# Reciprocal square roots with a GpSimd power as first guess in a hybrid attention layer

## The chip, the cores and the metric

The kernel runs on one core of a Trainium2 chip. The metric is device time in microseconds (us) of one execution, the median of several runs. The core's engines are PE (TensorE, matrix products; PEld is its weight load), DVE (VectorE), ACT (ScalarE), POOL (GpSimd) and SP (SyncE, which issues most DMAs). Each engine takes its own instructions strictly in the order in which the built program lists them, and waits on semaphores for the others.

## The reference

One inference step of one layer, on 2048 prompt tokens and 8 sequences of 16 sample tokens, 2176 tokens of width 1024 in all. The parts that matter here are its normalisations:

```
def rms_norm(x, g):
    y = x * rsqrt(mean(x * x) + EPS);  return y * g
def l2_norm(x):
    return x * rsqrt(sum(x * x) + EPS)

h = rms_norm(x, g_in);  all projections = h @ w_in
q_a = l2_norm(q_a) * 128 ** -0.5;  k_a = l2_norm(k_a)          # DeltaNet group, 4 heads of 128
o_a = rms_norm(gated_delta(q_a, k_a, v_a, ...), g_o) * silu(z_a)
q_b, k_b, q_m = rms_norm per head of 64;  k_i = rms_norm of 32  # sparse and memory attention, indexer
o_b = attention over the 256 best keys by indexer score
o_m = attention over 256 memory tokens
y = x + concat(o_a, o_b, o_m) @ w_out
```

## The kernel before

Tokens lie on the 128 partitions, in 17 tiles; tile 0 holds the sample tokens. The tiles form five groups of 4, 4, 3, 3 and 3 (`GROUPS`). The first part of the kernel, some 1600 us long, runs eleven streams beside one another: `projections` (h times the weights, in split precision, so three products each), their posts `n_post`, `idx_post` and `head_post`, the DeltaNet stages a, b and c (`delta_a`, `delta_b`, `delta_c`, one run per group and head, b and c in two or three units of tiles), `prep` (which scales the tokens by the norm `rstd`), weight loading and splitting, and the indexer with its top-k search (`topk`). The second part, to the end, runs sparse and memory attention and the output product.

The streams are generators. `weave` takes them in turn by a planned clock: each engine has a running time, a wrapper (`Paced`, whose call stands on line 169, which is why nearly every row of the profile names L169) adds a cost for each instruction, by engine and by width, and the stream with the earliest time goes next. A DVE step on a few elements is planned at some 71 ns, a POOL product on a few elements at some 155 ns. A framework then places buffers and semaphores, and schedules within that. So the order of all engines follows from planned costs, and another cost moves it.

The helper of this study is `rsqrt(y, x, pool, tag)` on lines 297 to 308. It works on very small operands: 128 partitions by 1 to 8 elements. It makes a first guess by integer arithmetic on the bits of x (the row writes int32) and two refinement steps, eight DVE instructions that each need the one before. It is called

- in `norms` (line 325, result `rstd`, scratch `x_b`), 5 times, once a group;
- in `n_post` (line 428, `nrs`, `n_b`), 30 times, for q and k of the sparse attention and q of the memory attention; the scaled `nraw` then goes to a POOL product, `nth`;
- in `idx_post` (line 468, `irs`, `i_b`), 10 times;
- in `topk` (line 553, `sdr`, `t_b`), 15 times, once for each searched tile, for a starting threshold;
- in `memory_keys` (lines 829 and 845), 3 times;
- in `delta_a` (line 1002, `drr`, `d_b`), 20 times, for the norms of k and q of a head; `rq` is q's part;
- in `delta_c` (line 1225, `fo`, `o_b`), 44 times, for the norm of the output `o`, from its sum of squares `sso`, into `Ao`, after squaring `rq`.

POOL's own work in the first part: `wl` and `mw` (low parts of split weights), `Lm` (masked copies of a triangular matrix, two buffers, so one must wait until PE has used an earlier one), `qn` (low part of the indexer's queries), `q`, `kdb`, `nth` and some memsets. In the first part DVE also makes `Z`, `Sst`, `kw`, `cv` for the DeltaNet chain on PE, `xr` and `xl` for the projections, `score` and the top-k steps for ACT.

Of the kernel before, what the change touches and what calls it, by code (L numbers as in the profile page):

```python
# [5 lines left out]
F32 = mybir.dt.float32  # L6
F32R = mybir.dt.float32r
BF = mybir.dt.bfloat16
I32 = mybir.dt.int32
AF = mybir.ActivationFunctionType  # L10
OP = mybir.AluOpType
# [5 lines left out]
EPS = 1e-6  # L17
# [189 lines left out]
def build(tc, nc, a):  # L207
# [3 lines left out]
    V, S, G, T = (Paced(e, n, log) for e, n in ((nc.vector, "V"), (nc.scalar, "S"), (nc.gpsimd, "G"), (nc.tensor, "T")))  # L211


    cpool = ctx.enter_context(tc.tile_pool(name="const", bufs=1))
# [79 lines left out]
    xh = xpool.tile([128, 8, MAXTOK], F32R, name="xh")  # L294
    xl = xpool.tile([128, 8, MAXTOK], F32R, name="xl")

    def rsqrt(y, x, pool, tag):

        t = pool.tile([128, x.shape[-1]], F32, name=tag + "_b", tag="rsq_b" + tag)
        V.tensor_scalar(y.bitcast(I32), x.bitcast(I32), -0.5, 1597463007.0, op0=OP.mult, op1=OP.add)  # L300
        V.tensor_tensor(t, y, y, op=OP.mult)
        V.tensor_tensor(t, t, x, op=OP.mult)
        V.scalar_tensor_tensor(t, t, -10.0 / 3, t, op0=OP.add, op1=OP.mult)
        V.scalar_tensor_tensor(y, t, 5.0, y, op0=OP.add, op1=OP.mult)
        V.scalar_tensor_tensor(t, y, -27.0 / 1024, y, op0=OP.mult, op1=OP.mult)
        V.tensor_tensor(t, t, x, op=OP.mult)
        V.scalar_tensor_tensor(y, t, 0.5625, y, op0=OP.add, op1=OP.mult)

    done = dict.fromkeys(("a", "b", "c", "i", "t", "s", "n", "na", "tp", "ta", "w", "end", "m", "k", "sv", "smp", "nm", "x", "xf", "bl", "sx"), 0)
    done["xf"] = 1  # L310
# [3 lines left out]
    def norms(gi, xp):  # L314
        g0, n = GROUPS[gi]
        ss = xp.tile([128, 5, 2], F32, name="ss")
        for t in range(n):
            for e in range(2):
                xt = np_.tile([128, 512], F32, name="nraw")
                nc.sync.dma_start(xt, a["x"][(g0 + t) * 128:(g0 + t + 1) * 128, e * 512:e * 512 + 512])  # L320
                S.activation(xt, xt, AF.Square, accum_out=ss[:, t, e:e + 1])
        sm = xp.tile([128, 5], F32, name="ssm")
        V.tensor_tensor(sm[:, :n], ss[:, :n, 0], ss[:, :n, 1], op=OP.add)
        V.tensor_scalar(sm[:, :n], sm[:, :n], 1.0 / D, EPS, op0=OP.mult, op1=OP.add)
        rsqrt(rstd[:, g0:g0 + n], sm[:, :n], spool, "x%d" % n)
        done["nm"] = gi + 1
# [81 lines left out]
    def n_post(pi, t0, m, raw, npool):  # L408
        rows = slice(t0 * 128, (t0 + m) * 128)
        if pi == 3:  # L410
            nc.sync.dma_start(dst3(a["vb"][rows, :]), raw)
            nc.sync.dma_start(dst3(v_d[rows, :]), raw)
            return
        sq = npool.tile([128, 2, 256], F32, name="nth")[:, :m]
        if pi >= 4:
            S.activation(sq, raw, AF.Tanh, scale=0.5)
            yield 1
            V.scalar_tensor_tensor(raw, sq, 1.0, raw, op0=OP.add, op1=OP.mult)
            c = (pi - 4) * 256
            nc.sync.dma_start(dst3(gate_d[rows, c:c + 256]), raw)  # L420
            return
        S.activation(sq, raw, AF.Square)
        yield 1
        ss = spool.tile([128, 8], F32, name="nss")[:, :m * 4]
        V.tensor_reduce(ss, sq.rearrange("p t (h d) -> p (t h) d", d=64), axis=AX.X, op=OP.add)
        V.tensor_scalar(ss, ss, 1.0 / 64, EPS, op0=OP.mult, op1=OP.add)
        rs = spool.tile([128, 8], F32, name="nrs")[:, :m * 4]
        rsqrt(rs, ss, spool, "n%d" % m)
        r3 = raw.rearrange("p t (h d) -> p (t h) d", d=64)
        V.tensor_tensor(r3, r3, rs[:, :, None].to_broadcast([128, m * 4, 64]), op=OP.mult)  # L430
        yield 1
        gn = gains[:, pi * 64:(pi + 1) * 64]
        G.tensor_tensor(sq.rearrange("p t (h d) -> p (t h) d", d=64), r3, gn[:, None, :].to_broadcast([128, m * 4, 64]), op=OP.mult)
        nc.sync.dma_start(dst3((qn_d, kn_d, qm_d)[pi][rows, :]), sq)
        if pi == 1:
            nc.sync.dma_start(dst3(a["kb"][rows, :]), sq)
# [20 lines left out]
    def idx_post(gi, t0, m, raw, sm, final):  # L457
# [8 lines left out]
        V.tensor_scalar(ms[:, :m], ss[:, :m], 1.0 / 32, EPS, op0=OP.mult, op1=OP.add)  # L466
        rs = spool.tile([128, 2], F32, name="irs")
        rsqrt(rs[:, :m], ms[:, :m], spool, "i%d" % m)
        kn = spool.tile([128, 2, 32], F32, name="ikn")
        V.tensor_tensor(kn[:, :m], k3, rs[:, :m, None].to_broadcast([128, m, 32]), op=OP.mult)  # L470
# [511 lines left out]
    def delta_a(gi, h, R, dp):  # L982

        g0, n = GROUPS[gi]
# [18 lines left out]
        rk, rq = rr[:, :n], rr[:, n:2 * n]  # L1003
        cc = dp.tile([128, 6], F32, name="dcc")
        V.tensor_tensor(cc[:, :n], beta[:, gs, h], rk, op=OP.mult)
        bp = dp.tile([128, 6], F32, name="dbp")
        V.tensor_tensor(bp[:, :n], cc[:, :n], rk, op=OP.mult)
        nbe = dp.tile([128, 6], F32, name="dnbe")
        V.scalar_tensor_tensor(nbe[:, :n], bp[:, :n], -1.0, egc[:, gs, h], op0=OP.mult, op1=OP.mult)
        yield 1  # L1010

        Lp = dp.tile([128, 4, 128], F32, name="Lp")
        at = dp.tile([128, 4, 128], F32, name="at")
        for lo, hi in units(gi):
            m = hi - lo
# [37 lines left out]
        def full(dt):  # L1053
            return dt[:n, :16384].rearrange("t (i j) -> i t j", j=128)
# [21 lines left out]
        X = dp.tile([128, 4, 128], F32, name="X")  # L1076
        Z = dp.tile([128, 4, 128], F32, name="Z")
# [2 lines left out]
            nc.sync.dma_start(diag(Zd)[t], Zs[8 * t:8 * t + 8])  # L1080
        nc.sync.dma_start(X[:, :n], full(Xd))
        nc.sync.dma_start(Z[:, :n], full(Zd))
        R.update(Lp=Lp, at=at, X=X, Z=Z, cc=cc, nbe=nbe, rq=rq)
        yield 6000.0

    def delta_b(gi, h, lo, hi, R, dp):
# [63 lines left out]
    def delta_c(gi, h, lo, hi, R, dp):  # L1150

        g0, n = GROUPS[gi]
        q, z = (R[x][:, :n * 128].rearrange("p (t c) -> p t c", c=128) for x in "qz")
        at, rq = R["at"], R["rq"]
        Zg, kd, cv, nw = R[lo]
        m = hi - lo
        smp = g0 + lo == 0
        shp = [128, m, 128]
        sso = dp.tile([128, 3], F32, name="sso")
# [59 lines left out]

        f = dp.tile([128, 3], F32, name="fo")  # L1220
        A = dp.tile([128, 3], F32, name="Ao")
        V.tensor_tensor(f[:, :m], rq[:, lo:hi], rq[:, lo:hi], op=OP.mult)
        V.tensor_tensor(A[:, :m], f[:, :m], sso[:, :m], op=OP.mult)
        V.tensor_scalar(A[:, :m], A[:, :m], 1.0 / 16384, EPS, op0=OP.mult, op1=OP.add)
        rsqrt(f[:, :m], A[:, :m], dp, "o%d" % m)
        V.scalar_tensor_tensor(f[:, :m], f[:, :m], 128.0 ** -0.5, rq[:, lo:hi], op0=OP.mult, op1=OP.mult)
        V.tensor_tensor(o, o, f[:, :m, None].to_broadcast(shp), op=OP.mult)
# [15 lines left out]
    dp = b1.enter_context(tc.tile_pool(name="dp", bufs=2))  # L1243
# [5 lines left out]
    def stage_a():  # L1249
        for n, (gi, h, R) in enumerate(heads):  # L1250
            yield from until(lambda: done["tp"] >= 4 * n + 2 and done["t"] > gi and (n < 2 or done["c"] >= through[n - 2]))
            yield 1
            yield from delta_a(gi, h, R, dp)
            done["a"] += 1
# [7 lines left out]
    def stage_c():  # L1262
        for j, (n, lo, hi) in enumerate(pieces_):
            yield from until(lambda: done["b"] > j and done["tp"] >= 4 * n + 4)
            yield from delta_c(*heads[n][:2], lo, hi, heads[n][2], dp)
            done["c"] += 1
# [15 lines left out]
    def t_step(n, j):  # L1282
        gi, h, R = heads[n]
        parts_ = ((("k", 1, 128), ("q", 0, 0)), (("v", 2, 0), ("z", 3, 128)))[j]

        def run(w):
            if j == 0 and n >= 2:
                yield from until(lambda: done["c"] >= through[n - 2])
            yield from head_proj(n, h, gi, w, parts_, R, hp)
        return pairs(a["w_t"][2 * h + j]), run  # L1290

    def n_step(gi, pi):
        return pairs(a["w_n"][pi]), lambda w: n_piece(gi, pi, w, np_)
# [4 lines left out]
    for gi in range(len(GROUPS)):  # L1298
        t = [[t_step(4 * gi + h, 0), t_step(4 * gi + h, 1)] for h in range(4)]
        n = [n_step(gi, pi) for pi in (1, 0, 2, 3, 4, 5)]  # L1300
# [652 lines left out]
```

## Time and profile before

| | |
|---|---|
| median of 3 runs | 2352.61 us (2351.39 to 2356.84) |
| profiled execution | 2355.36 us, span 2353.5 us |
| PE busy | 2096.8 us, 89% |
| DVE busy | 1651.6 us, 70% |
| ACT busy | 1292.9 us, 55% |
| POOL busy | 419.7 us, 18% |
| mean granted clock of PE | 0.946 |

Busy time of an engine is the time in which at least one of its instructions runs; small DVE instructions overlap, so the sum of their durations is more than that. The span runs from the first to the last instruction; the execution's own time is a little longer. The granted clock is that of PE as a share of full speed.

### The profile page before, as it was taken

To read this page: it belongs to the slowest core of one execution; us is meant where nothing else is said; L and a number is where in the kernel's file an instruction comes from. 1 tells how busy PE (TensorE), PEld (TensorE's weight loads), DVE (VectorE), ACT (ScalarE), POOL (GpSimd) and SP (SyncE) were. 2 spreads that over 40 slices of the span, in tenths; PEclk is the share of its full clock that TensorE was granted. 3 is DMA by queue.
4 is the path that set the end of the run, shared out by engine and by line. 5 is a ranking of instruction groups with operands and counts; after the bars stand their busy time and mean duration, and the time that the engine had idled before them with its cause. 6 is when DMAs were issued, how large, how long until landed. Compare 5 with 4: busy or idle time off the path is not lost.

```text
span 2353.5 us, 43495 instructions
## 1 busy us (share of the span) xinstructions
PE 2096.8 (89%) x14123; PEld 1645.1 (70%) x14123; DVE 1651.6 (70%) x6571; ACT 1292.9 (55%) x3193; POOL 419.7 (18%) x494
## 2 busy tenths in 40 slices
PE   4887989788899998999899999989999999799997
PEld 3755645677688887888788888756566555467665
DVE  4765655566888787899888996777567667554552
ACT  3454545455546565676666764467456656544552
POOL 3231413211121111111111021132111111111100
PEclk9887989788999998999899999999999999999998
DMA  7688667765544555656555555368788777653212
GB/s 230 177 242 224 214 147 212 196 233 192 198 159 161 183 176 197 206 196 218 181 204 203 198 202 201 117 211 262 246 249 272 246 238 249 189 165 101 91 48 69
DMA packets 323533, 453.25 MB, mean 193 GB/s; under 512 B 81760, under 2 KB 230880, under 8 KB 303840
## 3 DMA queue, kind: packets, MB, share of 16 engines
q1 hardware_dynamic: 322976, 449.32, 59.9%
q8 instruction: 114, 1.87, 0.3%
q0 software_dynamic: 320, 1.06, 0.2%
q14 instruction: 123, 1.01, 0.1%
HBM read 344.53 MB, written 105.75 MB: 191 GB/s over the span
## 4 chain that ended last, share of the span: by engine, by line


## 5 line engine op out<-in xcount | busy, mean ns | idle before, releaser
L169 PE MATMUL pp<-wh,xh 128*128 128x256 f32 (+1 forms) x952 | 290.0, 305 | 10.6 <-ACT v L169 4.5
L169 PE MATMUL pp<-wh,xl 128*128 128x256 f32 (+1 forms) x952 | 280.6, 295 | 1.5 <-DVE xl L169 1.4
L169 PE MATMUL pp<-wl,xh 128*128 128x256 f32 (+1 forms) x952 | 280.5, 295 | 1.3 <-POOL wl L169 1.2
L169 PE MATMUL pp<-xh,wh 128*128 128x384 f32 (+1 forms) x640 | 249.5, 390 | 5.6 <-ACT q L169 3.2
L169 ACT ACTIVATE relu<-pi 128x512 f32<-128x512 f32 (+3 forms) x340 | 183.4, 545 | 125.0 <-PE pi L169 67.1
L169 PE MATMUL pp<-xh,wl 128*128 128x384 f32 (+1 forms) x640 | 242.2, 379 | 2.3 <-DMA wl<-wd2l 1.7
L169 DVE SCALAR_TENSOR_TENSOR score<-relu,w,score 128x512 f32<-128x512 f32 (+3 forms) x304 | 221.7, 731 | 29.5 <-ACT relu L169 15.0
L169 PE MATMUL pp<-xl,wh 128*128 128x384 f32 (+1 forms) x640 | 241.9, 378 | 0.0
L169 PEld LDWEIGHTS pp<-wh,xh 128*128 128x128 f32 x952 | 186.5, 196 | 17.6 <-ACT v L169 4.8
L169 PEld LDWEIGHTS pp<-wl,xh 128*128 128x128 f32 x952 | 186.3, 196 | 5.8 <-issue 2.5
L169 PEld LDWEIGHTS pp<-wh,xl 128*128 128x128 f32 x952 | 185.6, 195 | 5.1 <-DVE xl L169 2.7
L169 ACT ACTIVATE junk<-score,tf 128x1024 bf16<-128x1024 f32 (+11 forms) x126 | 142.5, 1131 | 69.8 <-DVE tf L169 47.9
L169 POOL TENSOR_TENSOR Lm<-Lp,cf 128x256 f32<-128x256 f32 (+1 forms) x120 | 85.0, 709 | 335.6 <-PE pb L169 312.2
L169 PE MATMUL pi<-kstack,qst 128*128 128x512 f32 (+3 forms) x304 | 129.6, 434 | 13.9 <-ACT relu L169 10.9
L169 PEld LDWEIGHTS pp<-xh,wh 128*128 128x128 f32 x640 | 125.4, 196 | 18.3 <-ACT q L169 3.8
L169 PEld LDWEIGHTS pp<-xh,wl 128*128 128x128 f32 x640 | 125.1, 196 | 15.6 <-issue 2.5
L169 PE MATMUL py<-woh,mixh 128*128 128x512 f32 x272 | 123.8, 455 | 11.6 <-ACT mixh L169 10.8
L169 PEld LDWEIGHTS pp<-xl,wh 128*128 128x128 f32 x640 | 125.4, 196 | 10.6 <-issue 2.5
L169 PE MATMUL py<-woh,mixl 128*128 128x512 f32 x272 | 111.4, 410 | 4.7 <-POOL mixl L169 4.5
L169 POOL TENSOR_TENSOR wl<-wr,wh 128x512 fp32r<-128x512 f32 (+1 forms) x61 | 80.7, 1333 | 188.8 <-ACT wh L169 186.3
L169 PE MATMUL py<-wol,mixh 128*128 128x512 f32 x272 | 110.6, 406 | 0.0
L169 ACT ACTIVATE PT<-pt 128x512 f32<-128x512 f32 (+1 forms) x112 | 64.3, 577 | 79.3 <-PE pt L169 78.4
(417 smaller groups left out, 5497.6 us busy)
## 6 DMA issues: line engine op xcount, KB each, us to landing
skt<-in_kT SPq DMA_DIRECT2D x128, 256.0 KB
svt<-in_v SPq DMA_DIRECT2D x128, 256.0 KB
nraw<-in_x SPq DMA_DIRECT2D x34, 256.0 KB
xres<-in_x SPq DMA_DIRECT2D x34, 256.0 KB
part_d<-xres SPq DMA_DIRECT2D x34, 256.0 KB
xres<-part_d SPq DMA_DIRECT2D x34, 256.0 KB
out_y<-xres SPq DMA_DIRECT2D x34, 256.0 KB
mixr<-mixT_d SPq DMA_DIRECT2D x33, 256.0 KB
```

Source lines behind the costliest of these rows:

```text
L169: return f(*args, **kw)
```

## The change

`rsqrt` takes its first guess from a power on POOL, x to the -0.5, with a constant tile `mhalf` as second operand, and then makes one refinement step on DVE, three instructions. In `delta_c` the square of `rq`, which was taken again for every unit, is taken once a head in `delta_a` (`rq2`, with the factor 1/16384 in it) and handed on.

```
+    mhalf = cpool.tile([128, 1], F32, name="mhalf")
+    V.memset(mhalf, -0.5)
     def rsqrt(y, x, pool, tag):
         t = pool.tile([128, x.shape[-1]], F32, name=tag + "_b", tag="rsq_b" + tag)
-        V.tensor_scalar(y.bitcast(I32), x.bitcast(I32), -0.5, 1597463007.0, op0=OP.mult, op1=OP.add)
-        V.tensor_tensor(t, y, y, op=OP.mult)
+        G.tensor_tensor(y, x, mhalf.to_broadcast([128, x.shape[-1]]), op=OP.pow)
+        V.scalar_tensor_tensor(t, y, -0.5, y, op0=OP.mult, op1=OP.mult)
         V.tensor_tensor(t, t, x, op=OP.mult)
-        V.scalar_tensor_tensor(t, t, -10.0 / 3, t, op0=OP.add, op1=OP.mult)
-        V.scalar_tensor_tensor(y, t, 5.0, y, op0=OP.add, op1=OP.mult)
-        V.scalar_tensor_tensor(t, y, -27.0 / 1024, y, op0=OP.mult, op1=OP.mult)
-        V.tensor_tensor(t, t, x, op=OP.mult)
-        V.scalar_tensor_tensor(y, t, 0.5625, y, op0=OP.add, op1=OP.mult)
+        V.scalar_tensor_tensor(y, t, 1.5, y, op0=OP.add, op1=OP.mult)
...
     in delta_a, after the norms of a head
+        rq2 = dp.tile([128, 6], F32, name="drq2")
+        V.scalar_tensor_tensor(rq2[:, :n], rq, 1.0 / 16384, rq, op0=OP.mult, op1=OP.mult)
...
     in delta_c
-        V.tensor_tensor(f[:, :m], rq[:, lo:hi], rq[:, lo:hi], op=OP.mult)
-        V.tensor_tensor(A[:, :m], f[:, :m], sso[:, :m], op=OP.mult)
-        V.tensor_scalar(A[:, :m], A[:, :m], 1.0 / 16384, EPS, op0=OP.mult, op1=OP.add)
+        V.tensor_tensor(A[:, :m], rq2[:, lo:hi], sso[:, :m], op=OP.mult)
+        V.tensor_scalar(A[:, :m], A[:, :m], EPS, None, op0=OP.add)
         rsqrt(f[:, :m], A[:, :m], dp, "o%d" % m)
```

Since the wrapper prices other instructions now, the order of all engines is another one. Three places show what that means. In brackets stands whose semaphores an instruction waits for.

DVE at the norm of a DeltaNet output in `delta_c`, the eighth of the 44 (tiles of two): before, from the guess `fo<-Ao` on.

```order
L169 TENSOR_SCALAR fo<-Ao 128x2 [waits DVE_49]
L169 TENSOR_TENSOR o_b<-fo 128x2 [waits DVE_49]
L169 TENSOR_TENSOR o_b<-o_b,Ao 128x2 [waits DVE_49]
L169 SCALAR_TENSOR_TENSOR o_b<-o_b 128x2 [waits DVE_49]
L169 TENSOR_TENSOR Z<-Z,pb 128x128 [waits PE_49]
L169 SCALAR_TENSOR_TENSOR fo<-o_b,fo 128x2 [waits DVE_49]
L169 SCALAR_TENSOR_TENSOR o_b<-fo 128x2 [waits DVE_49]
L169 TENSOR_TENSOR o_b<-o_b,Ao 128x2 [waits DVE_49]
L169 SCALAR_TENSOR_TENSOR fo<-o_b,fo 128x2 [waits DVE_49]
L169 SCALAR_TENSOR_TENSOR fo<-fo,drr 128x2 [waits DVE_49]
L169 TENSOR_TENSOR o<-o,fo 128x256 [waits DVE_49,Activation_49]
```

The same norm on DVE now; the rows of `tmp`, `st` and `tf` are of a top-k search.

```order
L169 TENSOR_TENSOR Ao<-drq_3188,sso 128x2 [waits Activation_49]
L169 SCALAR_TENSOR_TENSOR tmp_3952<-tmp_3952,st_3942 128x1 [waits DVE_49]
L169 TENSOR_SCALAR Ao<-Ao 128x2 [waits DVE_49]
L169 TENSOR_TENSOR Z<-Z,pb 128x128 [waits PE_49]
L169 TENSOR_TENSOR tmp_3952<-tmp_3952,st_3942 128x1 [waits DVE_49]
L169 SCALAR_TENSOR_TENSOR o_b<-fo 128x2 [waits Pool_49]
L169 COPY_PREDICATED tf<-msk,tmp_3952 128x1 [waits DVE_49]
L169 TENSOR_TENSOR o_b<-o_b,Ao 128x2 [waits DVE_49]
L169 TENSOR_SCALAR tf<-tf 128x1 [waits DVE_49]
L169 SCALAR_TENSOR_TENSOR fo<-o_b,fo 128x2 [waits DVE_49]
L169 SCALAR_TENSOR_TENSOR fo<-fo,drr 128x2 [waits DVE_49]
L169 TENSOR_TENSOR o<-o,fo 128x256 [waits DVE_49,Activation_49]
```

Five dependent steps are gone; between `Ao` and the first refinement step, which now waits for POOL, stand two instructions of other streams.

POOL at the start of the program, before: split weights of the indexer (`wl`) and of the memory keys (`mw`).

```order
L169 TENSOR_TENSOR mw<-mraw,mw 128x512 [waits DMAHW7_49,Activation_49]
L169 TENSOR_TENSOR mw<-mraw,mw 128x512 [waits DMAHW3_49,Activation_49]
L169 TENSOR_TENSOR wl<-wr,wh 128x2x256 [waits DMAHW7_49,Activation_49]
L169 TENSOR_TENSOR wl<-wr,wh 128x8x48 [waits DMAHW0_49,Activation_49]
L169 TENSOR_TENSOR mw<-mraw,mw 128x512 [waits DMAHW1_49,Activation_49]
```

POOL there now:

```order
L169 TENSOR_TENSOR mw<-mraw,mw 128x512 [waits DMAHW7_49,Activation_49]
L169 TENSOR_TENSOR mw<-mraw,mw 128x512 [waits DMAHW3_49,Activation_49]
L169 TENSOR_TENSOR rstd<-ssm,mhalf 128x4 [waits DVE_49]
L169 TENSOR_TENSOR wl<-wr,wh 128x2x256 [waits DMAHW7_49,Activation_49]
L169 TENSOR_TENSOR wl<-wr,wh 128x8x48 [waits DMAHW0_49,Activation_49]
L169 TENSOR_TENSOR mw<-mraw,mw 128x512 [waits DMAHW1_49,Activation_49]
```

The power for the first token norm stands between two products that wait for ACT and a load.

POOL in the middle of the first part, around the 67th of the 120 `Lm` products, before:

```order
L169 TENSOR_TENSOR q<-q,er 128x256 [waits DVE_49,PE_49,Activation_49]
L169 TENSOR_TENSOR Lm<-Lp,cf 128x128 [waits PE_49,Pool_49]
L169 TENSOR_TENSOR Lm<-Lp,cf 128x128 [waits PE_49]
L169 TENSOR_TENSOR Lm<-Lp,cf 128x256 [waits PE_49] x2
L169 TENSOR_TENSOR q<-q,er 128x128 [waits PE_49,Activation_49]
L169 TENSOR_TENSOR qn<-qr,qn 128x8x32 [waits DMAHW0_49,Activation_49]
```

POOL around the same `Lm` now:

```order
L169 TENSOR_TENSOR Lm<-Lp,cf 128x128 [waits PE_49,Pool_49]
L169 TENSOR_TENSOR qn<-qr,qn 128x8x32 [waits PE_49,Activation_49]
L169 TENSOR_TENSOR Lm<-Lp,cf 128x128 [waits PE_49,Pool_49]
L169 TENSOR_TENSOR Lm<-Lp,cf 128x256 [waits PE_49,Pool_49]
L169 TENSOR_TENSOR fo<-Ao,mhalf 128x2 [waits DVE_49]
L169 TENSOR_TENSOR Lm<-Lp,cf 128x256 [waits PE_49]
L169 TENSOR_TENSOR irs<-ims,mhalf 128x2 [waits DVE_49]
```

Two powers stand behind products that wait for PE; of the 127 powers, 43 have an `Lm` right ahead of them and 11 a `qn`.

## Rows read from the trace of the kernel before

**Rows 1.** The page's first part: busy us (share of the span) xinstructions of each engine.
```profile
PE 2096.8 (89%) x14123; PEld 1645.1 (70%) x14123; DVE 1651.6 (70%) x6571; ACT 1292.9 (55%) x3193; POOL 419.7 (18%) x494
```
**Rows 2.** Windows: length, busy PE, PEld, DVE, ACT, POOL, clock, DMA share, GB/s.
```profile
600.00:1000.00 400.00, 366.65 (x2398) 332.24 (x2397) 336.45 (x1656) 232.28 (x592) 58.70 (x86) 0.96 0.54 180
1000.00:1480.00 480.00, 450.35 (x3008) 409.63 (x3007) 423.73 (x1976) 304.15 (x766) 70.89 (x110) 0.98 0.57 198
...
1600.00:2353.00 753.00, 696.33 (x5534) 465.53 (x5534) 439.56 (x1431) 391.29 (x951) 100.28 (x86) 0.98 0.58 185
```
**Rows 3.** Waits of PE: who waited for whom, us in total, times, longest.
```profile
PE pp L169 <- DVE xr L169: 9.0, 8, 2.8
PE pl L169 <- DVE o L169: 8.9, 10, 2.8
```
**Rows 4.** Windows of 10 us: three of eight slices, and the sum of the eight.
```profile
900.00:910.00 10.00, 7.90 (x30) 7.33 (x29) 9.45 (x72) 6.45 (x17) 0.95 (x1) 0.50 0.52 169
1130.00:1140.00 10.00, 5.92 (x33) 5.01 (x33) 9.93 (x60) 9.12 (x25) 0.77 (x1) 0.84 0.54 209
1140.00:1150.00 10.00, 5.86 (x17) 4.85 (x18) 9.72 (x52) 4.18 (x7) 0.87 (x1) 0.50 0.25 57
...
sum 80.00, PE 53.73 PEld 43.13 DVE 76.55 ACT 46.60 POOL 12.60; mean PE 6.72 PEld 5.39 DVE 9.57 ACT 5.82 POOL 1.57
```
**Rows 5.** One tile's instructions, `o_b`: ns min/median/max, first and last start, forms.
```profile
L169 DVE TENSOR_TENSOR o_b<-o_b,Ao x88: 106/153/1249, 262.7 to 1561.4; 128x2 f32<-128x2 f32 x48, 128x1 f32<-128x1 f32 x40
```
**Rows 6.** Timeline of DVE near 1202 and 1213 us: start, duration, instruction.
```profile
1201.91 0.14 DVE L169 TENSOR_TENSOR o_b<-o_b,Ao 128x1 f32<-128x1 f32 x1
1201.98 0.21 DVE L169 TENSOR_TENSOR Xs<-Xs,xt 24x63 f32<-24x63 f32 x1
...
1212.83 0.17 DVE L169 SCALAR_TENSOR_TENSOR d_b<-d_b 128x6 f32<-128x6 f32 x1
1213.03 0.17 DVE L169 SCALAR_TENSOR_TENSOR drr<-d_b,drr 128x6 f32<-128x6 f32 x1
```
**Rows 7.** Groups of POOL's instructions: xcount, busy us, mean ns, idle before.
```profile
L169 POOL TENSOR_TENSOR Lm<-Lp,cf 128x256 f32<-128x256 f32 x72 | 58.1, 808 | 211.8 <-PE pb L169 191.6 <-DVE fo L169 9.1 <-DVE o_b L169 8.7
...
L169 POOL TENSOR_TENSOR Lm<-Lp,cf 128x128 f32<-128x128 f32 x48 | 26.9, 561 | 123.8 <-PE pb L169 120.7 <-issue 2.0 <-DVE score L169 1.0
...
L169 POOL MEMSET Xs<- 32x16 f32 x20 | 2.4, 118 | 1.1
```
**Rows 8.** Timelines of DVE and POOL near 261 us.
```profile
261.43 1.13 DVE L169 SCALAR_TENSOR_TENSOR n_b<-n_b 128x8 f32<-128x8 f32 x1
...
261.25 1.27 POOL L169 TENSOR_TENSOR wl<-wr,wh 128x512 fp32r<-128x512 f32 x1 [0.94 <-ACT wh L169]
```
**Rows 9.** Timelines: DVE then POOL near 664 us, POOL then PE near 623.
```profile
663.96 0.69 DVE L169 TENSOR_TENSOR nraw<-nraw,nrs 128x512 f32<-128x512 f32 x1
...
664.73 1.75 POOL L169 TENSOR_TENSOR nth<-nraw,gains 128x512 f32<-128x512 f32 x1 [1.23 <-DVE nraw L169]
...
622.95 0.72 POOL L169 TENSOR_TENSOR qn<-qr,qn 128x256 fp32r<-128x256 f32 x1 [6.19 <-ACT qn L169]
...
623.73 0.69 PE L169 MATMUL pi<-cf,qn 128*128 128x128 f32 x2 [3.80 <-POOL qn L169]
```
**Rows 10.** Waits of POOL: us in total, times, longest.
```profile
POOL Lm L169 <- PE pb L169: 312.2, 97, 13.5
...
POOL qn L169 <- ACT qn L169: 176.5, 23, 21.6
```
**Rows 11.** Timelines of DVE and POOL at the start of the program.
```profile
30.78 0.16 DVE L169 SCALAR_TENSOR_TENSOR rstd<-x_b,rstd 128x4 f32<-128x4 f32 x1
30.97 4.75 DVE L169 TENSOR_SCALAR xr<-cf,rstd 128x128 f32<-128x128 f32 x4
...
16.75 2.49 POOL L169 TENSOR_TENSOR wl<-wr,wh 128x512 fp32r<-128x512 f32 x2 [12.13 <-ACT wh L169]
...
30.93 2.22 POOL L169 TENSOR_TENSOR wl<-wr,wh 128x512 fp32r<-128x512 f32 x2 [3.79 <-ACT wh L169]
```

More of the change, by code (lines that the diff above doesn't have):

```diff
@@ L1082, in delta_a @@
         nc.sync.dma_start(Z[:, :n], full(Zd))
-        R.update(Lp=Lp, at=at, X=X, Z=Z, cc=cc, nbe=nbe, rq=rq)
+        R.update(Lp=Lp, at=at, X=X, Z=Z, cc=cc, nbe=nbe, rq=rq, rq2=rq2)
         yield 6000.0
@@ L1153, in delta_c @@
         q, z = (R[x][:, :n * 128].rearrange("p (t c) -> p t c", c=128) for x in "qz")
-        at, rq = R["at"], R["rq"]
+        at, rq, rq2 = R["at"], R["rq"], R["rq2"]
         Zg, kd, cv, nw = R[lo]
```

## Prediction

> **What bounds the kernel now.** I read the engines' shares first, then their busy time by stage, then what PE waited for. PE is busy 89% of the span, DVE 70%, POOL 18% [rows 1]. By stage [rows 2]: from 600 to 1480 us, where projections, DeltaNet heads and top-k run together, PE is busy 817 of 880 us and DVE 760 of 880; after 1600 us PE has 92% and DVE 58%. So PE sets the end, DVE stands close behind it in the middle of the first part, and POOL is nearly free. What PE waits for by name is spread thin [rows 3]: its largest waits for DVE that follow this code are 8.9 us for `o` and 9.0 us for `xr`. Average shares hide one thing: in short stretches DVE is full and PE idles [rows 4]. In the three slices shown DVE is busy 9.4 to 10 us of 10 while PE has 5.9 to 7.9, and the granted clock is 0.50 to 0.84 of full speed there, at or above the lower of its two levels, 1.2 and 2.4 GHz. Of the 160 slices of 10 us before 1600 us, 38 have DVE at 9.5 us or more (each read from the same view as rows 4), 0.24 of them. That is my rate for turning DVE time into span: a microsecond of DVE counts in about a quarter of the places, since elsewhere PE is the later one.
>
> **The change part by part.** The helper `rsqrt` is called 127 times in the executed path: 5 token norms, 30 query/key norms, 10 index-key norms, 15 top-k deviations, 3 in the memory keys, 20 in `delta_a`, 44 in `delta_c`. Each call drops from 8 DVE steps to 3 and gains one POOL step. In `delta_c` 3 steps ahead of it become 2 (44 fewer), and `delta_a` gains 1 (20 more). Removed on net: 635 + 44 - 20 = 659 DVE instructions; one memset of `mhalf` is added at the start, where DVE waits for loads anyway.
>
> What a removed step is worth: its own duration is 0.15 us in the median [rows 5], but steps overlap. In a bare chain each starts 0.20 us after the one before; interleaved with other work the next instruction starts 0.07 us later [rows 6]. So 659 steps are worth between 46 us (0.07) and 132 us (0.20); I take 0.15, 99 us of DVE time, as both kinds occur and rows 5 lie between.
>
> What the power costs on POOL no row shows. Below, the memset of 32x16 takes 0.12 us; the smallest two-operand row, 128x128, 0.56 us mean, and 128x256 takes 0.81 [rows 7]; above, I put 1.27 us, the 128x512 product [rows 8]. I take 0.56: the operand is 1 to 8 elements wide, so fixed cost should rule, but a power is surely dearer per element than a product.
>
> What crossing engines costs: POOL's product `nth` starts 0.08 us after the end of the DVE step that it waits for (0.13 where it is less prompt; I use 0.13), and PE starts 0.06 us after POOL's `qn` [rows 9]; I take the same for DVE. A call then holds its chain for 0.13 + 0.56 + 0.06 = 0.75 us. DVE runs in order, so at the step that waits for POOL everything behind it waits too: the updates of `Z` and `Sst` that PE needs, top-k steps that ACT needs. What covers it is other work that stands between the producer and that step: in the new order the median is one DVE instruction, and 35 of 127 have none. I credit 0.15 us. Nor is all of that real cover, for a DVE step with two operands in SBUF stretches while POOL runs: `n_b` took 1.13 us instead of 0.15, ending with POOL's `wl` [rows 8]. So DVE stands still 0.60 us a call, 76 us in all; with 0.12 for the power 20 us, with 1.27 it is 166 us.
>
> POOL's queue: a power stands behind whatever was issued before it. 43 of the 127 stand right behind an `Lm` product that waits for PE, and 11 behind a `qn` that waits for ACT; in the trace POOL waited 3.2 us on average at `Lm` (312.2 us in 97 waits) and 7.7 at `qn` [rows 10]. That bounds it from above: if half of such an `Lm` wait falls on DVE, 43 x 1.6 = 69 us. From below: `nth` already stands where the power of the query/key norms will, and 25 of its 30 instances start within 0.15 us of their operand (all 30 read like rows 9; the mean is 0.23, the longest 2.1). I take 0.09 us a call, 11 us in all, since that is the same place and the same kind of wait.
>
> DVE's sum: -99 + 76 + 11 = -12 us; from -132 + 20 = -112 to -46 + 166 + 69 = +189. At 0.24 the -12 are -3 us of span.
>
> Latency, apart from load. In `delta_c` the chain up to `o` loses six steps at 0.20 and gains 0.75: 0.45 us shorter. PE waited for `o` 10 times [rows 3]; 10 x 0.45 = 4.5 us. At the very start the token norm stands alone on the path to the first projection: the steps of `rstd` run 0.20 apart up to 30.94 us and then `xr` follows [rows 11]. Five steps less and one power more: -1.00 + 0.75 = -0.25 us. POOL is idle then (its next `wl` begins at 30.93), so the power goes at once. Everything in the attention part stays as it is but for three top-k deviations. Sum: -3 - 4.5 - 0.25, about -8 us. The profiled execution took 2355.36 us (span 2353.5), 2.75 above the median 2352.61; taken off the median that is 2345 us.
>
> The Trainium skill, GPSIMD Engine Reference, section 4.1 Engine selection, speaks against the move: elementwise arithmetic belongs on VectorE, POOL being about twice as slow. Read on the 0.15 us step, that makes the power an estimated 0.30 us, below the row that I took, and the sum an estimated 2334 us, which lies inside the rival "more than the sum". No run here shows a power on either engine, and the rule names none, so the row stands.
>
> The weave of the streams is recomputed with other costs, so the order changes nearly everywhere in the first part. Landmarks (the last projection, the last state update, the first scores) keep their places within 1% of PE's queue, so I give this no sign, only width.
>
> **The rivals.** *A long power (slower).* Place: all 127 calls, mostly 600 to 1480 us, where DVE has least slack. Price with 1.27 us: 166 + 11 - 99 = +78 us of DVE, at 0.24 about +19 us: 2372. It decides from about 0.65 us, where 0.13 + 0.65 + 0.06 + 0.09 - 0.15 equals the 0.78 us that 99 us make per call. For it: nothing in the trace shows such an operation. Against: operands of 8 elements at most.
>
> *POOL's queue couples the engines (slower).* DVE waits for POOL, POOL for PE at `Lm`, and PE soon for DVE. Price: 58 us more than the 11, at 0.24 +14: 2359. For it rows 10; against it rows 9.
>
> *More than the sum (faster).* The full stretches dissolve. In eight slices of this kind, read together, PE is busy 53.73 of 80 us, so 26 idle; the lower clock costs 12 us in the three shown, and I put 20 for the eight [rows 4]. Half of both is 23 us: 2330. For it: the clock falls where PE idles. Against: only about 2 to 4 us of each such stretch of 20 to 30 us is `rsqrt` steps.
>
> *Covered (no change).* PE's own work hides both sides, 2352. For it: PE busy 94% in 1000 to 1480 us.
>
> *A first call that costs.* The first use of a new POOL routine could stall the token norm at the start; every microsecond there moves the first projection. For it nothing: POOL's first products took 2.49 us for two, as later ones [rows 11]. A stall of more than 5 us would bring the time back to about 2351. By the Trainium skill, GPSIMD Engine Reference, section 2.1 Instruction dispatch, the first call of a freshly loaded routine costs about 6 us; by that 2345 becomes an estimated 2351.
>
> *It doesn't do what it says.* If guess and one step were not exact enough, the top-k test would take the exact path and attention would run again, at least 753 us more [rows 2].
>
> **How the numbers follow.** Forecast, a small gain centred on 2345 (2338 to 2350): 0.34, of which 0.04 falls within 0.2% (4.7 us, about what a measurement can tell from no change). More than the sum 0.15. Covered 0.15. Long power 0.17. Queue 0.14. First call 0.04. Exact path 0.01. Faster: 0.30 + 0.15 = 0.45. Same: 0.04 + 0.15 + 0.04 = 0.23. Slower: 0.17 + 0.14 + 0.01 = 0.32. For 8 in 10 the range takes in 2330 with the width of the reordering below it, 2322, and the long power above, 2374; the forecast's own range is 2338 to 2350.
>
> **What the new profile would show.** Right: DVE's instructions down by 658 and its busy time by some 80 to 100 us; the power near 0.5 us; DVE waiting for POOL some 0.3 to 0.6 us a call; PE's wait for `o` below 5 us. Wrong: a power above 0.65 us, single DVE waits for POOL of several microseconds with an `Lm` or `qn` ahead, or PE's busy time and clock moved by the new order in places without any `rsqrt`.

## The result and the profile after

The changed kernel took 2391.51 us in the median of 4 runs (2381.39 to 2393.36), the kernel before on the same chip 2352.00 us (2347.55 to 2356.84). The measured ratio is 1.0145, 95% interval 1.0121 to 1.0168: some 34 us slower, outside the predicted range of 2322 to 2374 us. The two medians alone lie 39.5 us apart; all that follows goes by the ratio. The profiled execution took 2390.6 us, with a span of 2388.8 us.

The page's first part after, against [rows 1]: busy us (share of the span) and instructions of each engine.

```profile
PE 2091.3 (88%) x14123; PEld 1649.8 (69%) x14123; DVE 1589.2 (67%) x5913; ACT 1290.3 (54%) x3193; POOL 553.2 (23%) x621
```

DVE has 658 instructions and 62 us of busy time less, POOL 127 instructions and 134 us more, and PE has the same work in a span that is 35 us longer. The windows, against [rows 2] (length, then busy PE, PEld, DVE, ACT, POOL, then clock):

```profile
600.00:1000.00 400.00, 347.26 (x2231) 313.14 (x2230) 310.05 (x1363) 215.94 (x557) 97.16 (x118) 0.93 0.50 168
1000.00:1480.00 480.00, 437.50 (x2896) 403.23 (x2895) 397.25 (x1737) 300.84 (x746) 111.23 (x148) 0.96 0.56 194
```

From 600 to 1480 us PE lost 32 us of busy time (817.0 to 784.8), and the granted clock fell from 0.96 and 0.98 of full speed to 0.93 and 0.96. DVE, which looked full there, now looks freer: of the 160 slices of 10 us before 1600 us, 10 have it busy for 9.5 us or more, where there were 38. That is not slack. DVE stands still, waiting. Its waits for POOL, of which the kernel before had none (us in total, times, longest):

```profile
DVE n_b L169 <- POOL nrs L169: 41.2, 29, 2.9
DVE o_b L169 <- POOL fo L169: 24.7, 37, 1.4
DVE d_b L169 <- POOL drr L169: 23.2, 17, 2.9
DVE t_b L169 <- POOL sdr L169: 7.8, 13, 1.3
DVE x_b L169 <- POOL rstd L169: 5.2, 5, 1.7
DVE i_b L169 <- POOL irs L169: 4.9, 8, 1.6
```

They are 107 us in 109 waits, about 1 us each (three more, in the memory keys, add 2.6 us; all totals below are of these six). The cause of that size is the power (POOL's instructions that read `mhalf`: ns least/median/most, first and last start, forms):

```profile
L169 POOL TENSOR_TENSOR fo<-Ao,mhalf x44: 547/697/1228, 269.0 to 1613.1; 128x2 f32<-128x2 f32 x24, 128x1 f32<-128x1 f32 x20
L169 POOL TENSOR_TENSOR nrs<-nss,mhalf x30: 1001/1634/2136, 129.6 to 1451.2; 128x8 f32<-128x8 f32 x21, 128x4 f32<-128x4 f32 x9
L169 POOL TENSOR_TENSOR drr<-dms,mhalf x20: 1320/1632/2857, 112.5 to 1525.8; 128x6 f32<-128x6 f32 x12, 128x8 f32<-128x8 f32 x8
L169 POOL TENSOR_TENSOR sdr<-sd,mhalf x15: 536/548/552, 448.6 to 1989.8; 128x1 f32<-128x1 f32 x15
```

Its length goes with the number of elements: 0.55 us for one, 1.63 for eight. The 134 us that POOL gained are 1.05 us a call.

One place shows how that reaches PE, the timeline of the three engines near 1206 us (start, duration, instruction, idle before):

```profile
1203.77 0.16 DVE L169 TENSOR_SCALAR nss<-nss 128x8 f32<-128x8 f32 x1
1203.95 0.75 DVE L169 SCALAR_TENSOR_TENSOR score<-relu,w,score 128x512 f32<-128x512 f32 x1
...
1204.23 1.05 POOL L169 TENSOR_TENSOR Lm<-Lp,cf 128x256 f32<-128x256 f32 x1 [4.15 <-PE pb L169]
1204.71 0.71 PE L169 MATMUL pb<-Y,X 128*128 128x128 f32 x4
...
1205.25 1.63 POOL L169 TENSOR_TENSOR nrs<-nss,mhalf 128x8 f32<-128x8 f32 x1
...
1206.91 0.17 DVE L169 SCALAR_TENSOR_TENSOR n_b<-nrs 128x8 f32<-128x8 f32 x1 [2.21 <-POOL nrs L169]
1207.00 0.35 DVE L169 SCALAR_TENSOR_TENSOR Lp<-pa,dbp,e 128x128 f32<-128x128 f32 x1
1207.26 0.41 DVE L169 TENSOR_TENSOR Z<-Z,pb 128x256 f32<-128x256 f32 x1
...
1207.72 0.71 PE L169 MATMUL pb<-Z,Lm 128*128 128x128 f32 x4 [1.60 <-DVE Z L169]
```

The operand `nss` is ready at 1203.93. The power waits 1.3 us for POOL's `Lm`, then runs 1.63 us; DVE covers 0.75 us of that with `score` and stands for 2.21 us at `n_b`. Behind `n_b` in DVE's order stand `Lp` and `Z`, which have nothing to do with this norm, though the product that `Z` needs was done at 1205.42. PE waits 1.60 us for `Z`. In the kernel before PE waited for `Z` so, for `o` and `xr` as in [rows 3]:

```profile
PE pb L169 <- DVE Z L169: 7.6, 12, 1.3
```

and now:

```profile
PE pb L169 <- DVE Z L169: 24.1, 23, 3.1
...
PE pl L169 <- DVE o L169: 19.3, 16, 2.6
...
PE pp L169 <- DVE xr L169: 15.4, 4, 5.8
```

All of PE's waits that DVE ended came to 87.8 us before and 147.8 us now.

### The profile page after: what moved, and what is told of

The parts are those of the page before. It is cut to its first block, busy times and chain, and to the rows that moved or that the text cites. A ratio compares the mean times of both kernels' runs of the same rounds, so it can differ in the third digit from the quotient of the medians.

```text
span 2388.8 us, 42971 instructions
## 1 busy us (share of the span) xinstructions
PE 2091.3 (88%) x14123; PEld 1649.8 (69%) x14123; DVE 1589.2 (67%) x5913; ACT 1290.3 (54%) x3193; POOL 553.2 (23%) x621
## 4 chain that ended last, share of the span: by engine, by line
## 5 line engine op out<-in xcount | busy, mean ns | idle before, releaser
L169 POOL TENSOR_TENSOR mixl<-mixr,mixh 128x512 fp32r<-128x512 f32 x33 | 42.8, 1298 | 332.0 <-ACT mixh L169 262.3
```

What stands on the lines that cost most here:

```text
L169: return f(*args, **kw)
```

## The experiments

Ratios are to the kernel before on the same chip, with 95% intervals; 0.001 is 2.35 us. The intervals, some 0.003 to either side, leave a difference of two ratios uncertain by about 10 us. "The plan" is the set of costs by which `weave` orders the streams.

**The parts apart.** e1 keeps the old helper and takes only `rq2`; e2 takes only the new helper. Against the changed kernel:

```
e1   -  G.tensor_tensor(y, x, mhalf..., op=OP.pow) and the three steps
     +  the eight steps of the kernel before
e2   -  V.tensor_tensor(A[:, :m], rq2[:, lo:hi], sso[:, :m], op=OP.mult)
     -  V.tensor_scalar(A[:, :m], A[:, :m], EPS, None, op0=OP.add)
     +  V.tensor_tensor(f[:, :m], rq[:, lo:hi], rq[:, lo:hi], op=OP.mult)
     +  V.tensor_tensor(A[:, :m], f[:, :m], sso[:, :m], op=OP.mult)
     +  V.tensor_scalar(A[:, :m], A[:, :m], 1.0 / 16384, EPS, op0=OP.mult, op1=OP.add)
```

> Only the second part of the change: the square of rq once a head, and the old eight-step helper on DVE; no power on POOL. 24 DVE steps fewer. The power as cause: nothing of the loss is here, 24 x 0.15 = 3.6 us of DVE less, 2348 to 2353 us. The redrawn order as cause: the planner's costs differ a little here too, so a shift of some 10 us in either direction would be seen already.

> Only the first part: the power on POOL and one step on DVE, with the old square taken again in delta_c. The power as cause (its duration, 1.05 us mean in the trace of the changed kernel, or its place in POOL's queue): all of the loss is here, 2385 to 2397 us, a little over the changed kernel for 44 more short DVE steps in delta_c. If the once-a-head square does harm (its tile lives longer, delta_a is longer): below 2380.

e1: 1.0071 (1.0047 to 1.0095). e2: 1.0263 (1.0232 to 1.0293), and its DVE waits 110 us for POOL. The kernel with the power alone loses 62 us, more than the whole change, but e1 has 24 DVE steps fewer than the kernel before, no wait for POOL to speak of (0.3 us), and is 17 us slower: something else counts too. Each of the two has its own order, so they do not divide the loss.

**The power made short.**

```
-        G.tensor_tensor(y, x, mhalf.to_broadcast(...), op=OP.pow)
+        if tag[0] in "xit":   # token norms, indexer keys, top-k: as in the changed kernel
+            G.tensor_tensor(y, x, mhalf.to_broadcast(...), op=OP.pow)
+        else:
+            G.tensor_tensor(y, x, C("zc")[:, 31:32].to_broadcast(...), op=OP.mult)
```

> The changed kernel with a POOL product by a constant in the place of the power in 97 of the 127 calls (query/key norms, delta_a, delta_c, memory keys), same operands, same waits, nearly the same order; those norms are then wrong, all else stays. Long power: the product on 1 to 8 elements should take 0.15 to 0.5 us, so DVE's waits for POOL (some 110 us) shrink by 50 us or more and 25 us or more of the 39 us come back, 2352 to 2366 us. POOL's queue (standing behind products that wait for PE or ACT): the waits stay as they are, 2380 to 2392. Redrawn order: 2380 to 2392 as well.

0.9895 (0.9860 to 0.9930): all of the loss came back and 25 us more. The product takes 0.20 us in the median, at one element as at eight, and DVE's waits fell from 107 to 36 us. Its instructions for two of the tiles:

```profile
L169 POOL TENSOR_TENSOR fo<-Ao,cf x44: 190/196/720, 263.7 to 1550.3; 128x2 f32<-128x2 f32 x24, 128x1 f32<-128x1 f32 x20
...
L169 POOL TENSOR_TENSOR nrs<-nss,cf x30: 198/204/706, 128.7 to 1393.3; 128x8 f32<-128x8 f32 x21, 128x4 f32<-128x4 f32 x9
```

DVE's waits for them:

```profile
DVE o_b L169 <- POOL fo L169: 8.1, 20, 0.9
DVE n_b L169 <- POOL nrs L169: 5.8, 14, 1.4
```

The queue and the crossing are the same in both kernels, and so is nearly all of the order: of PE's 14123 products, in the order of the traces, 14099 stand at the same place as in the changed kernel. So it is the power's own length. The norms are wrong in e3, but that is not what makes it fast: e9 and e12 below, with right norms and no wait, take the same time.

**The power doubled**, the second without a cost in the plan.

```
         G.tensor_tensor(y, x, mhalf.to_broadcast([128, x.shape[-1]]), op=OP.pow)
+        nc.gpsimd.tensor_tensor(y, x, mhalf.to_broadcast([128, x.shape[-1]]), op=OP.pow)
```

> The changed kernel with each power issued twice, the second planned at nothing, so in the order of the changed kernel. It measures the price of a longer power: 127 calls by 1.05 us are 134 us more of DVE standing still. At 0.24 us of time per us of that, +32 us (ratio 1.028); at 0.8, +107 us (ratio 1.06). If PE's work hid the powers (loss from the order alone): ratio below 1.02.

1.0763 (1.0727 to 1.0800), 145 us over the changed kernel. DVE's waits for POOL went from 107 to 222 us with the same instructions on DVE:

```profile
DVE n_b L169 <- POOL nrs L304: 86.1, 30, 4.7
DVE d_b L169 <- POOL drr L304: 51.3, 20, 4.4
DVE o_b L169 <- POOL fo L304: 50.4, 44, 2.1
```

So 115 us of standing still cost 145 us, 1.26 per us; from the product to the power it was 71 us for 59, 0.83. For waits the rate of 0.24 is refuted. That the first is above 1 goes with PE's clock: the mean granted clock is 0.927 in e7 against 0.944 in the changed kernel, and PE is busy 37 us longer with the same products (e7's page line):

```profile
PE 2128.7 (84%) x14123; PEld 1680.8 (67%) x14123; DVE 1584.9 (63%) x5913; ACT 1289.5 (51%) x3193; POOL 673.0 (27%) x748
```

**The plan alone.** e4 runs the old instructions under the costs of the new ones, e9 the same with `rq2`; e5 the new instructions under the old costs; e6 the new ones with the measured price of the power; e15 is the kernel before with one price changed.

```
e4, e9   log.append(("G", 150 + 2.1 * n)); log.extend([("V", 70 + n / 0.96)] * 3)    # and the eight steps unlogged
e5       log.extend([("V", 70 + n / 0.96)] * 8)                                     # and the power and three steps unlogged
e6       log.append(("G", 390 + 160.0 * n))                                        # and the power unlogged
e15      t = (130 if op == "scalar_tensor_tensor" and n > 16 else 75) + n / 0.96    # before: 70
```

> The instructions of the kernel before (eight DVE steps, the square taken each time), but the planner is given the costs of the new ones, so the streams are woven about as in the changed kernel; no power. Redrawn order as cause: 2375 to 2392 us. The power as cause: 2348 to 2358, no loss beyond the scatter of an order.

> The instructions of the changed kernel, but the planner is given the costs of the old ones, so the streams are woven about as in the kernel before. A long power: the loss stays in this order too; with the rate that the product in the power's place showed (time fell 59 us where DVE's waits for POOL fell by 75, 0.8 us per us), 107 us of waits less 62 of DVE's busy time cost 45 x 0.8 = 36 us, ratio 1.010 to 1.025. Redrawn order: ratio 0.995 to 1.005. At the rate of the prediction, 0.24, the ratio is about 1.005.

> The changed kernel, with the planner told what the power takes in its trace, 390 + 160 ns per element, in place of some 155 ns. If a planner that knows the price puts other work between the power and the step that waits: DVE's waits for POOL fall below 80 us and the ratio to 1.000 to 1.010. If the wait is one of DVE's own order, which the planner's clock does not model to the single step: the ratio stays within 1.008 to 1.025.

> The old eight DVE steps, woven as the new ones, which gave 0.9947 to the kernel before, and the square once a head as well: 24 DVE steps fewer than there, 3.6 us of DVE, and a chain to the norm of the output that is one step shorter. At 0.8 us per us of DVE: ratio 0.992 to 0.996. If the square once a head was what cost 0.7% by itself: above 1.000. If the order's scatter rules: anywhere from 0.99 to 1.007.

> The kernel before with one planned cost changed: a small DVE step is planned at 75 ns and its width instead of 70. No instruction is added or removed; the streams are woven in another order. If the redrawn order matters as e1, e4 and e9 suggest: a ratio up to 0.01 from 1 in either direction. If it is nearly neutral and those three differ for other reasons: 0.998 to 1.002.

e4: 0.9947 (0.9924 to 0.9970). e5: 1.0297 (1.0264 to 1.0331). e6: 1.0292 (1.0245 to 1.0339). e9: 0.9908 (0.9879 to 0.9937). e15: 0.9943 (0.9918 to 0.9968). Three things follow. The new order was no cause of the loss: with old steps it is a gain of 12 us (e4), or 22 with `rq2` (e9). All 127 powers together lose in every order tried (e2, e5, e6, e14), and the changed kernel's own was the mildest: under the old plan they and `rq2` cost 70 us, under the new one the powers cost 56 (1.0145 against 0.9908). And the order alone weighs as much as the change: e1 and e9 have the same instructions and differ only in the planned costs, yet lie 0.0163 apart, 38 us; in e15 one planned price, 5 ns higher, moved the kernel before by 13 us. The page line of e1:

```profile
PE 2103.9 (89%) x14123; PEld 1653.6 (70%) x14123; DVE 1653.5 (70%) x6547; ACT 1290.8 (54%) x3193; POOL 423.4 (18%) x494
```

and of e9:

```profile
PE 2085.2 (89%) x14123; PEld 1644.1 (70%) x14123; DVE 1645.4 (70%) x6547; ACT 1288.5 (55%) x3193; POOL 417.7 (18%) x494
```

That a planner with the right price of the power (e6) does not help I had not expected: DVE's waits for POOL fell only to 98 us, and the time rose. e2, e5 and e6, and e10 below, came out slower than anything that was expected for them.

**By width, and POOL's load by itself**, all under the plan of the changed kernel. e11 and e13 have the power in some of the calls and the old steps in the others; e12 has the old steps everywhere and the power beside them, into unread columns of `mhalf`.

```
e11  +  if int(x.shape[-1]) <= 2:    # the power and three steps
     +  else:                        # the eight steps
e13  +  if int(x.shape[-1]) > 2:
e12  +  k = min(int(x.shape[-1]), 7)
     +  nc.gpsimd.tensor_tensor(mhalf[:, 1:1 + k], x[:, :k], mhalf[:, :1].to_broadcast([128, k]), op=OP.pow)
```

> The plan of the changed kernel; the power only in the 70 calls on 1 or 2 elements (0.55 to 0.77 us in the trace), the old steps in the 57 wider ones. Long power, by its width: these calls cost about what they save (38 us of waits against 70 x 5 x 0.095 = 33 us of busy time), so ratio within 0.007 of the same plan with old steps only (0.9908): 0.988 to 0.999. POOL's queue: the narrow calls of the output norm are the ones that stand behind Lm products, so the loss is here: 1.005 or more.

> The counterpart: the power only in the 57 calls on 4 to 8 elements (1.0 to 1.8 us in the trace), old steps in the 70 narrow ones, the plan of the changed kernel. Long power, by its width: 71 us of waits against 57 x 5 x 0.095 = 27 us of busy time, +44 us on the same plan with old steps: ratio 1.003 to 1.015. POOL's queue: these stand mostly behind nothing that waits long, ratio below 1.000.

> Old eight DVE steps, the plan of the changed kernel, the square once a head, and beside them the 127 powers on POOL (on up to 7 elements) into a tile that nobody reads. If what costs is that DVE stands still for the power: ratio 0.985 to 0.997, as without the powers (0.9908). If what costs is that POOL is busier (it stretches DVE steps that read two operands, and its products come later): 1.005 or more.

e11: 0.9943 (0.9904 to 0.9982), with 34 us of waits. e13: 1.0133 (1.0098 to 1.0169), with 68. Against e9 that is +8 us for 70 narrow calls and +53 for 57 wide ones, together 61 of the 56 that all of them cost. e12: 0.9908 (0.9875 to 0.9942), the same as e9, though POOL is busy 122 us more (its page line):

```profile
PE 2074.8 (89%) x14123; PEld 1635.5 (70%) x14123; DVE 1655.5 (71%) x6548; ACT 1290.5 (55%) x3193; POOL 539.7 (23%) x621
```

POOL may run the powers for nothing, within some 10 us, as long as nobody waits for them; DVE's busy time is 10 us longer beside them, and the span is not.

**Wait, later result, or DVE's time?** e10 leaves the refinement out; e14 gives the turn away between power and first step; e16 is e9 with the old steps made twice.

```
e10  -  the three steps on V
     +  log.extend([("V", 70 + int(x.shape[-1]) / 0.96)] * 3)
e14     G.tensor_tensor(y, x, mhalf..., op=OP.pow)
     +  yield 1
e16  +  for _ in range(2):           # around the eight steps
```

> The changed kernel without the refinement step: the power is the result; 381 DVE steps fewer, planned as before, each call's chain some 0.5 us shorter; the norms have the power's own accuracy. By busy time they are worth 0.095 us each (the change took 62 us of busy time with 658 steps), 36 us. If the time follows DVE at about 1 us per us, as the doubled power showed: ratio 0.995 to 1.002. At 0.24: 1.010.

> The changed kernel, but the helper gives its turn away after it has issued the power (not in the 5 token norms), so that the planner puts other streams' work on DVE between the power and the first step. If the loss is DVE standing still in its own order: its waits for POOL fall from 107 us to below 50 and the ratio to 0.985 to 1.002. If it is that the norm's result comes later: the ratio stays at 1.010 or more, since each result comes later still. The plan is another one, which alone may move it by 0.8% in either direction.

> Old steps, the square once a head and the plan of the changed kernel (0.9908), with the eight steps made twice, one after the other, the second eight planned at nothing: no POOL. Each norm's result comes 1.0 to 1.6 us later (8 steps at 0.13 to 0.20), more than with one power, and DVE gets 1016 steps more, some 95 us of busy time at 0.095 each. If what costs is DVE standing still with other work queued behind: other streams' steps go between these, and only the busy time counts, 0.24 x 95 = 23 us, ratio 0.995 to 1.006. If the later result or DVE's time itself is what costs: like the doubled power at 1 us per us, 90 us or more, ratio 1.025 or more.

e10: 1.0146 (1.0109 to 1.0184). Against the changed kernel DVE has 43 us less busy time, each norm comes some 0.5 us sooner, the waits for POOL are as before (108 us), and so is the time. e14: 1.0265 (1.0228 to 1.0302), and it settles nothing: the waits for POOL fell only to 98 us, because the framework put the first step back: in the median two DVE instructions stand between the operand and it, where there was one. e16: 1.0206 (1.0171 to 1.0240), 70 us over e9, for 112 us more of DVE's busy time. The page line of e10:

```profile
PE 2086.0 (88%) x14123; PEld 1647.0 (69%) x14123; DVE 1545.7 (65%) x5532; ACT 1291.9 (54%) x3193; POOL 553.4 (23%) x621
```

and of e16:

```profile
PE 2098.9 (88%) x14123; PEld 1649.5 (69%) x14123; DVE 1757.1 (73%) x7563; ACT 1293.4 (54%) x3193; POOL 417.6 (17%) x494
```

That lies between the two expectations: DVE's work costs as well, 0.63 us per us when it is added. It is not standing still alone that counts: PE's waits for DVE, 81 us in e9, are 124 us in e16.

The nine kernels of one plan, side by side (us against e9 is the difference of the ratios times 2352). The plan is the same, the built order only in e3: there 14099 of PE's 14123 products stand at the same place as in the changed kernel, in the others 6469 (e16) to 9207 (e7).

| kernel | DVE busy | waits for POOL | ratio | us against e9 |
|---|---|---|---|---|
| e9, old steps | 1645 | 0 | 0.9908 | 0 |
| e12, unread power | 1656 | 0 | 0.9908 | 0 |
| e16, old steps twice | 1757 | 0 | 1.0206 | +70 |
| e3, short product | 1586 | 36 | 0.9895 | -3 |
| e11, narrow powers | 1616 | 34 | 0.9943 | +8 |
| e13, wide powers | 1620 | 68 | 1.0133 | +53 |
| changed kernel | 1589 | 107 | 1.0145 | +56 |
| e10, no refinement | 1546 | 108 | 1.0146 | +56 |
| e7, power twice | 1585 | 222 | 1.0763 | +201 |

Pairs with nearly the same busy time price the wait: e3 to the changed kernel 0.83, e11 to e13 1.3, the changed kernel to e7 1.26 us per us. Pairs with the same wait price the work: e9 to e16 0.63, e10 to the changed kernel 0 (within 10 us). The last pair misleads. A least-squares fit to all nine, with e9 as zero, gives 1.04 us for each us of waits and 0.65 for each us of DVE's busy time; it meets eight of the nine within 10 us, and the changed kernel alone lies 20 us below it. From e9 to e10 there are 108 us of waits more and 99 us of work less for +56 us: at 1.04, the work taken away gave back 0.57 per us.

## Why the prediction was wrong, step by step

- **The power's price** is the first step that failed. I took 0.56 us, from the smallest two-operand row [rows 7], with the reason that fixed cost rules on 1 to 8 elements. It is 1.05 us a call, above the 0.65 us from which, by the prediction itself, the sign turns. The reasoning held for a product (0.20 us at all widths), not for a power, which grows with each element. The rival "long power" had the mechanism, and its bound, 1.27 us, held the mean; its time, 2372, stopped short of the measured one because it used the same rate of 0.24.
- **The sum of waits** came out near: 76 + 11 = 87 us were put down, 107 measured. With the true length the same working gives 1.09 x 127 + 11 = 149, so the cover was better than the 0.15 us credited. **The queue** was 0.18 us a call, not 0.09: from the end of the step that makes the operand to the power's start the median is 0.08 us, the mean 0.26, and 27 of the 127 took over 0.3 (22 us beyond the crossing). The rival of coupled queues did not come: no wait for POOL exceeds 2.9 us.
- **What the removed steps give**: 99 us were put down, DVE's busy time fell by 62. I priced starts in a chain, but part of each was already covered by other streams' steps: the durations of all DVE instructions together fell by 112 us, the time with at least one of them running by only 62.
- **The rate of 0.24** is the second step that failed, and the larger one. With the measured waits and busy time, +45 us of DVE at 0.24 are +11 us. Measured is +34, of which the plan and `rq2` gave -22 (e9), so the power cost 56. Counting the slices in which DVE is full asks when DVE has no gap at all. Standing still costs 0.8 to 1.3, as PE's next operand is among what stands behind; a gap on DVE in the trace of before was mostly a wait of its own (580 of its 702 us idle were waits for PE and ACT), not room for another. For work the rate was too low as well: 0.63 where it was added, about 0.65 over the nine kernels.
- **The order** was given no sign, and rightly, but too little width: the forecast's own range, 2338 to 2350, allowed 6 us; the same instructions in other orders lie up to 38 us apart.
- **Latency**: PE's wait for `o` was to fall below 5 us and rose from 8.9 to 19.3. At the start the token norm was to come 0.25 us sooner; `xr` begins at 35.62 us instead of 30.97 [rows 11]. Of these 4.65 us, 1.70 are the operand `ssm`, which is ready later (31.05 us, before 29.35); the norm's own chain is 2.95 us longer. The power itself starts at once, but pushes POOL's `wl` and `mw` onto the three refinement steps, which then take some 1 us each instead of 0.16:

```profile
31.13 1.03 POOL L169 TENSOR_TENSOR rstd<-ssm,mhalf 128x4 f32<-128x4 f32 x1 [3.26 <-DVE ssm L169]
32.14 2.20 POOL L169 TENSOR_TENSOR wl<-wr,wh 128x512 fp32r<-128x512 f32 x2
32.20 1.22 DVE L169 SCALAR_TENSOR_TENSOR x_b<-rstd 128x4 f32<-128x4 f32 x1 [1.15 <-POOL rstd L169]
...
33.45 0.92 DVE L169 TENSOR_TENSOR x_b<-x_b,ssm 128x4 f32<-128x4 f32 x1
34.31 1.25 POOL L169 TENSOR_TENSOR mw<-mraw,mw 128x512 fp32r<-128x512 f32 x1
34.40 1.19 DVE L169 SCALAR_TENSOR_TENSOR rstd<-x_b,rstd 128x4 f32<-128x4 f32 x1
35.62 0.87 DVE L169 TENSOR_SCALAR xr<-cf,rstd 128x128 f32<-128x128 f32 x4
```

In the kernel before, POOL's `wl` ran beside the four `xr` steps instead, and these took 4.75 us [rows 11] against 0.87 now. So most of the delay is made up: the first projection product begins at 41.97 us instead of 40.52, 1.45 us later.

- **The first call** cost nothing of its own: this first power took 1.03 us, as later ones of its width. The Trainium skill, GPSIMD Engine Reference, section 2.1 Instruction dispatch, adds some 6 us to the first call of a freshly loaded routine; the trace shows no such stall, and no run here shows whether an earlier execution had already loaded the power. The prediction's estimate from section 4.1 Engine selection of the Trainium skill's GPSIMD Engine Reference, 0.30 us for a power, is too low by a factor of 2 to 6; the section's row speaks of add, mul and max.

What stays open: whether DVE's waits can be filled by order (e14 did not get other work in between), why the changed kernel lies some 20 us better than the other eight kernels of its plan would have it, and what in an order makes it a good one.

**A version that beats both** came out of it: e9, the old steps with `rq2` under the other plan, 0.9908 of the time before, about 22 us faster. Most of that is its order: e4 has 12 us of it with the old instructions alone, the other 9 are within the noise, and e1, with e9's instructions, is slower than the kernel before.

## What to carry to other kernels

Price a new operation by an operation of its own kind: a power is not a product, and its price per element can rule even at eight elements. Keep waits and work apart in the sum: a step that waits for another engine holds all that is queued behind it, and here a microsecond of that cost about a microsecond of the whole, while a microsecond of removed work gave back some 0.65. Where a planner sets the order, run the old instructions under the new order too; here the order alone weighed as much as the change.

## What the runs showed of the hardware

A POOL power takes 0.55 us on one element a partition and 1.63 us on eight, about 0.16 us more for each; a POOL product there takes 0.20 us at any of these widths (medians). 127 powers that nobody waits for (on up to seven elements) cost no time that can be told from none, within some 10 us (e12), though they run in 122 us of POOL's time beside DVE. A microsecond in which DVE stands still for POOL cost 0.8 to 1.3 us of the whole in this kernel, and a microsecond of DVE work 0.65.
